# Spreading a value projection over the attention heads that use it, with shorter softmax and norm arithmetic around it

## The chip, the cores and the metric

The kernel runs on one core of one Trainium2 chip. The metric is the device time of one execution in microseconds (us). A core has a matrix engine (TensorE, PE in the profile, with its weight loads as PEld), a vector engine (VectorE, DVE), a scalar engine for table functions (ScalarE, ACT), a general engine (GpSimd, POOL) and a queue that issues the DMA transfers (SyncE, SP). TensorE writes its sums into PSUM, which has 8 banks; VectorE and ScalarE read them from there. Each engine runs its own list of instructions in a fixed order and waits where an instruction's inputs or its output buffer are not ready.

## The reference, cut to what matters

The program is two transformer blocks of the first kind, then one of a second kind, for 512 tokens of width 1024 in float32. The change is in the attention of the second kind, and in one helper that the very first mixer uses too. From the second kind:

```python
xn = rmsnorm_2(h, norm1_w[l])
proj = xn @ w_in[l]
qd, kd, vd, qc, kc, vc, gd, gc = jnp.split(proj, IN_SPLITS, axis=-1)
# differential attention: 8 heads, two maps each, one value of width 128 per head
def probs(qq, kk):
    s = jnp.einsum('bqhd,bkhd->bhqk', qq, kk).astype(f32) * scale + bias
    return jax.nn.softmax(jnp.where(allowed, s, -jnp.inf), axis=-1)
a = probs(qblk[..., 0, :], k1) - lam * probs(qblk[..., 1, :], k2)
o = a @ v                                   # per head
o = rmsnorm_2(o, subln_w) * (1.0 - lam_init) # norm over the head's 128 values
# chunk attention: 8 heads of width 64, each chunk sees itself and the 8 before it
p = jax.nn.softmax(s, axis=-1)
```

Then both outputs are gated, projected and added to the residual, and a retrieval stage (`peer`) follows.

## The kernel before

Every projection is done in float32 by splitting both operands into a high and a low part: a unit of weights (128 x 1024) is loaded by SP (line 236), cast on ScalarE (line 248), its remainder taken on VectorE (line 249), and three TensorE matmuls make each product. The units lie in memory in the order in which the program uses them (`_weight_units`), so a change of order in the program comes with one there. Two helpers use them:

- `ws` (lines 324 to 334) computes one transposed 128 x 512 tile, 24 matmuls of 512 columns into one PSUM bank (lines 320 to 322). In the second mixer the bank is one of the two called `mm`, in turn. Queries and keys are made so.
- `xs` (lines 336 to 353) computes 256 columns for all 512 tokens: two units, 96 matmuls of 256 columns (lines 350 to 352), into two banks at once, both of which are open until the last matmul. `xs_to` (line 355) then copies them out with four ScalarE instructions (line 359), scaled by the row norm `rcol`. Values are made so.

PSUM holds two banks each of `mm`, `pz`, `pa` and `ps`. Attention uses `pz` for the logits (line 975), `ps` for transposes and `pa` for a head's output.

`mixer_2` (line 909) first makes all 1024 columns of the differential values with `xs_to(v, 1024)` (line 951), on `pa` and `pz` in turn. Then a list of generators runs in `pipeline` (line 192): at most `DW` = 3 at a time, a new one at every third step (`DG` = 3). The list follows `ORDER`: eight `diff_head`, one `chunk_values` (two steps of `xs_to` on the `pz` banks for the 512 chunk values), four `chunk_pair`. A `diff_head` makes its query and key (`qk`, line 955) in its first step. In each of four more it makes the logits of 128 queries (line 976), adds the bias and takes the row maximum in one VectorE instruction (line 985), negates the maximum (line 988), takes the exponential with its row sum on ScalarE (line 990), a reciprocal (line 991), combines the two maps (lines 1033 and 1034), and, one step late, transposes the result (line 999), copies it (line 1000) and multiplies it by the values (line 1007). `head_norm` (line 693) closes the head: squares on ScalarE (line 700), `rsqrt` (line 361: 12 small VectorE instructions, a bit pattern as first guess and three Newton steps), scaling (line 707), transposes (line 450). It is used by the four heads of the first mixer (`mixer_ab`) as well.

The order on each engine is not written out: a scheduler places ready instructions, and the program's order decides between them. ScalarE's function tables are loaded by an instruction that the toolchain puts where it is needed; the program names a table set once, in `setup` (line 438), ahead of `mixer_ab`.

Of the kernel before, what the change touches and what calls it, by code (L numbers as in the profile page):

```python
# [35 lines left out]
DW, DG, AG = 3, 3, 5  # L36
MR, KEEP = 2, 20
QB, QK, BB, EB = 2, 2, 4, 7
ORDER = 'ddddddddvcccc'
WIDE = ['mm', 'mm', 'pz', 'pz', 'pa', 'pa']  # L40
G_MIX0, G_FFN0, G_PLE0, G_MIX1, G_FFN1, G_PLE1, G_N1, G_N2 = range(8)

# [31 lines left out]
def _weight_units(i):  # L74
    us = []
    ab = i['ab_w_in'][0]
    fq = _interleave(_ws_units(ab[:, 2048:2560]), _ws_units(ab[:, 1536:2048]),
                     _ws_units(ab[:, 0:512]), _ws_units(ab[:, 512:1024]))
    gs = _xs_units(ab[:, 3072:3584], 256)
    us += gs[:2] + fq[:4] + gs[2:]  # L80
    us += _xs_units(ab[:, 1024:1536], 256)
    us += _xs_units(ab[:, 2560:3072], 256)
    us += fq[4:]
    us += _ws_units(i['ab_w_out'][0])

    def ffn(l):
        r = []
        for a, b in PIECES:
            r.extend(_interleave(_ws_units(i['ffn_up'][l], range(a, b)),
                                 _ws_units(i['ffn_up'][l], range(NF + a, NF + b))))  # L90
            r.extend(_ws_units(i['ffn_down'][l], None, a, b))
        return r

    def ple(l):
        pr = _pack(_ws_units(i['ple_proj'][l]), 4)
        ga = _ws_units(i['ple_gate'][l])
        return [pr[0]] + ga[:4] + [pr[1]] + ga[4:]

    us += ffn(0) + ple(0)
    cw = i['c_w_in'][0]  # L100
    us += _xs_units(cw[:, 1280:1536], 256)
    k_cols = cw[:, 1024:1280]
    q_idx = np.concatenate([np.arange(64) + 64 * (8 * P + 4 * a + g)
                            for P in range(2) for g in range(4) for a in range(2)])
    kt = _ws_units(k_cols)
    qt = _ws_units(cw[:, q_idx])
    us += [kt[0], kt[1]] + qt
    us += _ws_units(i['c_w_out'][0][q_idx, :])
    us += ffn(1) + ple(1)
    w2 = i['w_in_2'][0]  # L110
    us += _xs_units(w2[:, 2048:3072], 256)
    diff = _interleave(_ws_units(w2[:, 0:1024]), _ws_units(w2[:, 1024:2048]))
    values = _xs_units(w2[:, 4096:4608], 256)
    chunk = _interleave(_ws_units(w2[:, 3072:3584]), _ws_units(w2[:, 3584:4096]))
    for kind in ORDER:
        part, n = {'d': (diff, 2), 'v': (values, len(values)), 'c': (chunk, 2)}[kind]
        us += part[:n]
        del part[:n]
    gd = _ws_units(w2[:, 4608:5632])
    gc = _ws_units(w2[:, 5632:6656])  # L120
    bd = _ws_units(i['w_branch_diff_2'][0])
    bc = _ws_units(i['w_branch_chunk_2'][0])
    for m in range(8):
        us += [gd[m], gc[m], bd[m], bc[m]]
    us += _ws_units(i['w_out_2'][0])
    us += _ws_units(i['peer_wq_2'][0])
    return us
# [132 lines left out]
class Kernel:  # L260
# [100 lines left out]
    def rsqrt(self, src, n, scale):  # L361

        nc = self.nc
        new = lambda name, dtype=F32: self.sm.tile([128, 8], dtype, name=name)[:, :n]
        ms, iy = new("rq_m"), new("rq_i", I32)
        nc.vector.tensor_scalar(ms, src, scale, EPS, op0=ALU.mult, op1=ALU.add)
        nc.vector.tensor_scalar(iy, ms.bitcast(I32), 1, None, op0=ALU.logical_shift_right)
        nc.vector.tensor_scalar(iy, iy, -1, 0x5F3759DF, op0=ALU.mult, op1=ALU.add)
        y = iy.bitcast(F32)
        for r in range(3):  # L370
            t, yn = new("rq_t"), new("rq_y")
            nc.vector.tensor_mul(t, y, y)
            nc.vector.scalar_tensor_tensor(t, t, -0.5, ms, op0=ALU.mult, op1=ALU.mult)
            nc.vector.scalar_tensor_tensor(yn, t, 1.5, y, op0=ALU.add, op1=ALU.mult)
            y = yn
        return y


    def norm_k(self, k, g, first=False, to=None):
# [313 lines left out]
    def head_norm(self, tmp, po, gain, y, scale=None):  # L693

        nc = self.nc
        o = tmp.tile([128, T], F32, name="fp")
        ss = tmp.tile([128, 4], F32, name="hn_s")
        for tb in range(4):
            s = slice(tb * 128, tb * 128 + 128)
            nc.scalar.activation(o[:, s], po[:, s], AF.Square, accum_out=ss[:, tb:tb + 1],  # L700
                                 scale=1.0 if scale is None else scale[:, tb:tb + 1])
        r = self.rsqrt(ss, 4, 1.0 / 128)
        if scale is not None:
            nc.vector.tensor_mul(r, r, scale)
        for tb in range(4):
            s = slice(tb * 128, tb * 128 + 128)
            nc.vector.scalar_tensor_tensor(o[:, s], po[:, s], r[:, tb:tb + 1], gain[:, tb, :],
                                           op0=ALU.mult, op1=ALU.mult)
        self.transpose4(o, self.yh[:, y], self.yl[:, y])
# [199 lines left out]
    def mixer_2(self):  # L909
# [3 lines left out]
        with ExitStack() as outer:  # L913
# [3 lines left out]
            with ExitStack() as st:  # L917
# [30 lines left out]
                v = self.const([128, 4, 1024], "h")  # L948
                v2 = one.tile([128, 4, 512], F32, name="v2")
                self.norm_end()  # L950
                self.xs_to(v, 1024)

                kz = self.zeros(one, QB)

# [22 lines left out]
                        pl.append(ps)  # L977
                    return pl

                def probs(pl, tb, bias, r):  # L980

                    n = 128 * (tb + 1)
                    e = tmp.tile([128, T], F32, name="e", bufs=EB)
                    mx = tmp.tile([128, 1], F32, name="mx", bufs=8)
                    nc.vector.tensor_tensor_reduce(out=e[:, :n], in0=pl[:, :n], in1=bias[:, T - n:], scale=1.0,
                                                   scalar=-3.0e38, op0=ALU.add, op1=ALU.max, accum_out=mx)
                    ng = tmp.tile([128, 1], F32, name="ng", bufs=8)
                    nc.vector.tensor_scalar(ng, mx, -1.0, None, op0=ALU.mult)
                    z = tmp.tile([128, 1], F32, name="z", bufs=10)
                    nc.scalar.activation(e[:, :n], e[:, :n], AF.Exp, bias=ng, accum_out=z)  # L990
                    nc.vector.reciprocal(r, z)
                    return e[:, :n], z

                def turned(e, tb):
                    n = 128 * (tb + 1)
# [23 lines left out]
                def diff_head(h):  # L1019
                    q, k = qk()  # L1020
                    bias = tmp.tile([128, T], F32, name="bias", bufs=BB)
                    nc.vector.tensor_scalar(bias, nd, 2.0 ** -(h + 1), None, op0=ALU.mult)
                    yield
                    po = self.pa.tile([128, T], F32, name="pa")
                    last = None

                    r4 = tmp.tile([128, 4], F32, name="r4", bufs=3)
                    for tb in range(4):
                        r2 = tmp.tile([128, 1], F32, name="r", bufs=8)
                        pl = logits(q, k, tb)  # L1030
                        e1, z1 = probs(pl[0], tb, bias, r4[:, tb:tb + 1])
                        e2, _ = probs(pl[1], tb, bias, r2)
                        nc.vector.scalar_tensor_tensor(r2, r2, nlam, z1, op0=ALU.mult, op1=ALU.mult)
                        nc.vector.scalar_tensor_tensor(e1, e2, r2, e1, op0=ALU.mult, op1=ALU.add)
                        if last is not None:
                            values(po, *last, slice(h * 128, h * 128 + 128))
                        last = (e1, tb)
                        yield
                    values(po, *last, slice(h * 128, h * 128 + 128))
                    self.head_norm(tmp, po, sb4, h, r4)  # L1040

                def chunk_values():
                    for c in range(0, 512, 256):
                        self.xs_to(v2[:, :, c:c + 256], 256, "pz")
                        yield

                def chunk_pair(hp):
                    q, k = qk()
                    biases = []
                    for a in range(2):  # L1050
                        bias = tmp.tile([128, T], F32, name="bias", bufs=BB)
                        nc.sync.dma_start(bias, self.i['chb'][2 * hp + a])
                        biases.append(bias)
                    yield
                    po = self.pa.tile([128, T], F32, name="pa")
                    last = None
                    for tb in range(4):
                        pl = logits(q, k, tb)
                        es = []
                        for a in range(2):  # L1060
                            r = tmp.tile([128, 1], F32, name="r", bufs=8)
                            e, _ = probs(pl[a], tb, biases[a], r)
                            nc.vector.tensor_scalar(e, e, r, None, op0=ALU.mult)
                            es.append(e)
                        if last is not None:
                            values2(po, *last, hp * 128)
                        last = (es, tb)
# [1 line left out]
                    values2(po, *last, hp * 128)  # L1069
                    self.split(y2h[:, hp], y2l[:, hp], po)  # L1070

                parts = {'d': map(diff_head, range(8)), 'v': iter([chunk_values()]), 'c': map(chunk_pair, range(4))}
                pipeline([next(parts[kind]) for kind in ORDER], DW, DG)
                self.h = self.const([128, KD, T], "h")
                for a in range(KD):
                    nc.sync.dma_start(self.h[:, a, :], hd[a])
# [380 lines left out]
```

## Time and profile before

| what | us |
|---|---|
| median of 3 runs (3294.6 to 3304.15) | 3296.83 |
| the profiled execution, its own time | 3298.76 |
| its span in the trace | 3296.7 |
| TensorE busy in it | 3172.2 (96%) |
| VectorE busy | 2333.6 (71%) |
| ScalarE busy | 1457.9 (44%) |

The mean granted TensorE clock of the execution is 0.988 of full speed. The second mixer's attention lies between about 1440 and 1790 us. A busy share of TensorE is a modelled one: a matmul that waits in the pipeline counts as busy, so the number of matmuls in a stretch says more than the share.

### The profile page before, as it was taken

How to read it: one execution, taken by the hardware profiler on the slowest of the kernel's cores; microseconds unless marked ns; L12 is line 12 of the kernel's file. 1: busy time of each engine (PE TensorE's matmuls, PEld its weight loads, DVE VectorE, ACT ScalarE, POOL GpSimd, SP SyncE). 2: the span in 40 equal slices, each digit the busy share in tenths (PEclk: the TensorE clock that was granted, in tenths of full speed). 3: DMA queues.
4: the chain of work that ended last, by engine and by line, in shares of the span. 5: the costliest groups of instructions: out<-in, count | busy, mean ns of one | idle time of the engine just before them, and what ended most of it. 6: DMA issues, size and time to landing. Idle time of an engine off the chain costs nothing.

```text
span 3296.7 us, 44324 instructions
## 1 busy us (share of the span) xinstructions
PE 3172.2 (96%) x16121; PEld 2663.3 (81%) x16121; DVE 2333.6 (71%) x4667; ACT 1457.9 (44%) x2606; POOL 642.0 (19%) x640
## 2 busy tenths in 40 slices
PE   8998999999999999999799999999999999889998
PEld 7876877878778778798587888999999898667786
DVE  7687746566666466667855457999999788788654
ACT  5565323333444233345655233366767433233333
POOL 4234100022230000220000020021245444333000
PEclk9999999999999999999899999999999999999999
DMA  3211222223112222232131333567799999999762
GB/s 117 71 52 59 91 95 90 96 90 115 39 40 90 96 87 98 91 118 77 42 100 60 97 103 104 165 235 273 258 330 340 371 336 333 344 350 358 255 200 83
DMA packets 202762, 523.48 MB, mean 159 GB/s; under 512 B 17968, under 2 KB 91312, under 8 KB 201008
## 3 DMA queue, kind: packets, MB, share of 16 engines
q1 hardware_dynamic: 165680, 386.42, 34.8%
q0 software_dynamic: 36864, 134.23, 11.2%
q8 instruction: 127, 2.08, 0.3%
q14 instruction: 91, 0.75, 0.1%
HBM read 474.71 MB, written 45.88 MB: 158 GB/s over the span
## 4 chain that ended last, share of the span: by engine, by line
PE 85%; DVE 9%; DMA 2%; ACT 2%; issue 2%; POOL 0%; SPq 0%; DVEq 0%; ACTq 0%; POOLq 0%
PE mm L322 11%; PE mm L320 11%; PE mm L321 11%; PE pz L1363 5%; PE pa L1363 5%; PE ps L1363 5%; PE pz L322 4%; PE pz L320 4%; PE pz L321 4%; PE pa L322 4%; PE pa L320 4%; PE pa L321 4%; DVE wlo L249 2%; PE ps L1293 1%; DMA u<-in_pu,e 1%
## 5 line engine op out<-in xcount | busy, mean ns | idle before, releaser
L248 ACT CAST whi<-wr 128x1024 fp32r<-128x1024 f32 (+2 forms) x435 | 448.9, 1034 | 812.5 <-PE mm L321 338.9
L249 DVE TENSOR_TENSOR wlo<-wr,whi 128x1024 fp32r<-128x1024 f32 (+2 forms) x435 | 554.4, 1276 | 174.8 <-ACT whi L248 172.0
L322 PE MATMUL mm<-yh,wlo 128*128 128x384 f32 (+1 forms) x1260 | 450.0, 358 | 11.9 <-DVE wlo L249 11.4
L320 PE MATMUL mm<-yh,whi 128*128 128x384 f32 (+1 forms) x1260 | 449.2, 357 | 6.8 <-ACT whi L248 3.5
L321 PE MATMUL mm<-yl,whi 128*128 128x384 f32 (+1 forms) x1260 | 447.3, 355 | 0.0
L322 PEld LDWEIGHTS mm<-yh,wlo 128*128 128x128 f32 x1260 | 238.3, 189 | 33.9 <-DVE wlo L249 18.1
L320 PE MATMUL mm<-xh,whi 128*128 128x512 f32 x652 | 260.1, 401 | 4.7 <-DVE q L958 3.4
L321 PE MATMUL mm<-xl,whi 128*128 128x512 f32 x652 | 260.8, 400 | 0.0
L322 PE MATMUL mm<-xh,wlo 128*128 128x512 f32 x652 | 260.2, 400 | 0.0
L320 PEld LDWEIGHTS mm<-yh,whi 128*128 128x128 f32 x1260 | 238.1, 189 | 25.8 <-ACT whi L248 5.9
L321 PEld LDWEIGHTS mm<-yl,whi 128*128 128x128 f32 x1260 | 238.3, 189 | 15.5 <-DVE yl L287 0.4
L1147 POOL DMA_INDIRECT u<-in_pv,e x128 | 176.0, 1375 | 239.7 <-DVE hacc L1154 131.2
L1147 POOL DMA_INDIRECT u<-in_pu,e x128 | 166.8, 1303 | 209.7 <-DVE hid L1151 119.4
L286 ACT CAST ah<-a 128x384 fp32r<-128x384 f32 x128 | 65.5, 513 | 229.4 <-PE ps L1363 136.4
L1154 DVE SCALAR_TENSOR_TENSOR hacc<-u,hid,hacc 128x1024 f32<-128x1024 f32 x128 | 163.7, 1279 | 0.6
L1151 DVE CUSTOM_DVE_ANT_0 u<-u,xt 128x1024 f32<-128x1024 f32 x128 | 155.0, 1222 | 10.0 <-DMA u<-in_pu,e 10.0
L320 PEld LDWEIGHTS mm<-xh,whi 128*128 128x128 f32 x652 | 122.5, 189 | 36.6 <-DVE q L958 3.6
L322 PEld LDWEIGHTS mm<-xh,wlo 128*128 128x128 f32 x652 | 123.0, 189 | 30.4 <-issue 1.6
L321 PEld LDWEIGHTS mm<-xl,whi 128*128 128x128 f32 x652 | 123.0, 189 | 28.8 <-issue 1.0
L287 DVE TENSOR_TENSOR al<-a,ah 128x384 fp32r<-128x384 f32 x128 | 71.0, 556 | 103.3 <-ACT ah L286 94.9
L742 POOL MEMSET un<- 128x2 f32 x88 | 8.6, 99 | 663.2 <-DVE cv L748 605.2
L1289 DVE TENSOR_SCALAR o<-io,tr 128x128 f32<-128x128 f32 x384 | 109.3, 358 | 0.1
(495 smaller groups left out, 7646.6 us busy)
## 6 DMA issues: line engine op xcount, KB each, us to landing
wr<-in_wall SPq DMA_DIRECT2D x256, 512.0 KB, 3.3
wr<-in_ut SPq DMA_DIRECT2D x116, 512.0 KB, 5.2
xh<-in_pv SPq DMA_DIRECT2D x72, 512.0 KB, 5.7
wr<-in_pv SPq DMA_DIRECT2D x56, 512.0 KB, 5.5
G<-Gd SPq DMA_DIRECT2D x32, 768.0 KB, 8.4
Hd<-hg SPq DMA_DIRECT2D x84, 192.0 KB, 3.4
hg<-Hd SPq DMA_DIRECT2D x84, 192.0 KB, 6.0
wr<-in_wall SPq DMA_DIRECT2D x32, 448.0 KB, 3.3
```

The source lines that it names most:

```text
L248: k.nc.scalar.copy(hi[:, :ln], r)
L249: k.nc.vector.tensor_tensor(lo[:, :ln], r, hi[:, :ln].bitcast(F32), op=ALU.subtract)
L286: self.nc.scalar.copy(hi, src)
L287: self.nc.vector.tensor_sub(lo, src, hi.bitcast(F32))
L320: mm(ps, w[0], x[0], start=first, stop=False)
L321: mm(ps, w[0], x[1], start=False, stop=False)
L322: mm(ps, w[1], x[0], start=False, stop=last)
L1147: tc.keep_in_program_order(nc.gpsimd.indirect_dma_start(out=u, out_offset=None, in_=self.i[table], in_offset=bass.IndirectOffsetOnAxis(ap= ...
L1151: nc.vector.tensor_tensor_reduce(out=u, in0=u, in1=xt, scale=1.0, scalar=0.0, op0=ALU.mult, op1=ALU.add, accum_out=hid[:, j:j + 1])
L1154: nc.vector.scalar_tensor_tensor(hacc[:, 0], u, hid[:, j:j + 1], hacc[:, 0], op0=ALU.mult, op1=ALU.add)
L1289: nc.vector.tensor_scalar(o2[:, j], io, tr[:, 1, t + j:t + j + 1], tr[:, 2, t + j:t + j + 1], op0=ALU.is_equal, op1=ALU.mult)
L1363: mm(accs[b][c], w[:, ts], r[:, c * 512:c * 512 + 512], start=n == 0 and r is hi and w is ah, stop=n == 127 and w is al)
```

## The change

The differential values are no longer made ahead: every second `diff_head` makes 256 columns, those of itself and the next head, right after its query and key, on the two `mm` banks. Every second `chunk_pair` does the same for the chunk values, and the generator `chunk_values` goes. The units lie in the new order. The line at 985 now yields the negated logits and the negated maximum (scale -1, minimum), so line 988 goes and the exponential takes scale -1. Reciprocals are taken once for four row sums (`r4`) or for two (chunk pairs). `head_norm` uses a new `rsqrt_ln`, with logarithm and exponential on ScalarE for the first guess and one Newton step.

```diff
+    for part, vals, n in ((diff, dv, 8), (chunk, values, 4)):
+        for h in range(n):
+            us += part[2 * h:2 * h + 2]
+            if h % 2 == 0:
+                us += vals[h:h + 2]
...
+    def rsqrt_ln(self, src, n, scale):
+        nc = self.nc
+        new = lambda name: self.sm.tile([128, 8], F32, name=name)[:, :n]
+        ms, y, t, r = new("rq_m"), new("rl_y"), new("rq_t"), new("rq_y")
+        nc.vector.tensor_scalar(ms, src, scale, EPS, op0=ALU.mult, op1=ALU.add)
+        nc.scalar.activation(y, ms, AF.Ln)
+        nc.scalar.activation(y, y, AF.Exp, scale=-0.5)
+        nc.vector.tensor_mul(t, y, y)
+        nc.vector.scalar_tensor_tensor(t, t, -0.5, ms, op0=ALU.mult, op1=ALU.mult)
+        nc.vector.scalar_tensor_tensor(r, t, 1.5, y, op0=ALU.add, op1=ALU.mult)
+        return r
...
-        r = self.rsqrt(ss, 4, 1.0 / 128)
+        r = self.rsqrt_ln(ss, 4, 1.0 / 128)
...
-                self.xs_to(v, 1024)
...
-                def probs(pl, tb, bias, r):
+                def probs(pl, tb, bias, z):
...
-                    mx = tmp.tile([128, 1], F32, name="mx", bufs=8)
-                    nc.vector.tensor_tensor_reduce(out=e[:, :n], in0=pl[:, :n], in1=bias[:, T - n:], scale=1.0,
-                                                   scalar=-3.0e38, op0=ALU.add, op1=ALU.max, accum_out=mx)
                     ng = tmp.tile([128, 1], F32, name="ng", bufs=8)
-                    nc.vector.tensor_scalar(ng, mx, -1.0, None, op0=ALU.mult)
-                    z = tmp.tile([128, 1], F32, name="z", bufs=10)
-                    nc.scalar.activation(e[:, :n], e[:, :n], AF.Exp, bias=ng, accum_out=z)
-                    nc.vector.reciprocal(r, z)
-                    return e[:, :n], z
+                    nc.vector.tensor_tensor_reduce(out=e[:, :n], in0=pl[:, :n], in1=bias[:, T - n:], scale=-1.0,
+                                                   scalar=3.0e38, op0=ALU.add, op1=ALU.min, accum_out=ng)
+                    nc.scalar.activation(e[:, :n], e[:, :n], AF.Exp, scale=-1.0, bias=ng, accum_out=z)
+                    return e[:, :n]
...
+                    if h % 2 == 0:
+                        self.xs_to(v[:, :, h * 128:h * 128 + 256], 256, "mm")
                     yield
...
-                        e1, z1 = probs(pl[0], tb, bias, r4[:, tb:tb + 1])
-                        e2, _ = probs(pl[1], tb, bias, r2)
+                        e1 = probs(pl[0], tb, bias, z1)
+                        e2 = probs(pl[1], tb, bias, z2)
+                        nc.vector.reciprocal(r2, z2)
...
                     values(po, *last, slice(h * 128, h * 128 + 128))
+                    nc.vector.reciprocal(r4, z4)
                     self.head_norm(tmp, po, sb4, h, r4)
...
+                    if hp % 2 == 0:
+                        self.xs_to(v2[:, :, hp * 128:hp * 128 + 256], 256, "mm")
...
+                        es = [probs(pl[a], tb, biases[a], z[:, a:a + 1]) for a in range(2)]
+                        nc.vector.reciprocal(z, z)
...
-                pipeline([next(parts[kind]) for kind in ORDER], DW, DG)
+                pipeline([diff_head(h) for h in range(8)] + [chunk_pair(hp) for hp in range(4)], DW, DG)
```

## Rows read from the trace of the kernel before

**Rows 1.** Second mixer's windows: length, busy (instructions) PE, PEld, DVE, ACT, POOL, clock, DMA.
```profile
1440.00:1484.00 44.00, 44.00 (x371) 43.59 (x371) 14.41 (x36) 16.40 (x27) 0.00 (x0) 1.00 0.28 94
1484.00:1540.00 56.00, 56.00 (x268) 46.33 (x267) 39.82 (x111) 31.26 (x68) 0.00 (x0) 1.00 0.26 85
1540.00:1610.00 70.00, 62.41 (x312) 51.00 (x310) 55.99 (x200) 43.80 (x106) 0.00 (x0) 0.95 0.19 61
1610.00:1650.00 40.00, 25.47 (x130) 19.87 (x131) 35.61 (x171) 27.09 (x90) 0.00 (x0) 0.79 0.06 20
...
1700.00:1790.00 90.00, 90.00 (x530) 69.02 (x530) 55.50 (x191) 53.04 (x128) 0.00 (x0) 1.00 0.19 59
```

**Rows 2.** Windows of tile mm's instructions alone: the same columns without POOL.
```profile
1610.00:1650.00 40.00, 0.00 (x0) 0.00 (x0) 1.36 (x2) 0.00 (x0) 0.79 0.06 20
```

**Rows 3.** Groups by form on PE, 1540 to 1700: count, busy, mean, idle before.
```profile
L320 PE MATMUL mm<-xh,whi 128*128 128x512 f32 x80 | 33.2, 415 | 3.5 <-DVE q L958 3.4
...
L1007 PE MATMUL pa<-h,eT 128*128 128x128 f32 x140 | 21.5, 286 | 1.7 <-ACT eT L1000 1.4
L350 PE MATMUL pz<-whi,xh 128*128 128x256 f32 x64 | 19.6, 307 | 2.1 <-DVE mx L985 2.0
...
L999 PE MATMUL ps<-ident,e 128*128 128x128 f32 x70 | 13.3, 293 | 0.0
L306 PE MATMUL pz<-kt,qh 128*128 128x256 f32 x24 | 8.0, 342 | 6.6 <-DVE mx L985 6.6
L306 PE MATMUL pz<-kt,qh 128*128 128x512 f32 x13 | 6.9, 530 | 4.5 <-DVE mx L985 3.5 <-ACT v L359 1.0
...
L450 PE MATMUL ps<-ident,fp 128*128 128x128 f32 x28 | 6.5, 325 | 0.0
...
L306 PE MATMUL pz<-kt,qh 128*128 128x384 f32 x12 | 5.0, 418 | 4.8 <-DVE mx L985 4.8
```

**Rows 4.** Chain that ended last, in time: start, us of the chain, work.
```profile
1486.19 0.23 PE mm L320
...
1535.11 0.89 PE pa L1007 x8
```

**Rows 5.** Groups on DVE and ACT, 1440 to 1790.
```profile
L991 DVE RECIPROCAL r<-z 128x1 f32<-128x1 f32 x96 | 14.9, 159 | 12.2 <-ACT e L990 11.4
L988 DVE TENSOR_SCALAR ng<-mx 128x1 f32<-128x1 f32 x96 | 13.3, 147 | 0.5
...
L963 DVE TENSOR_TENSOR q<-mm,rbc 128x512 f32<-128x512 f32 x12 | 8.2, 687 | 5.2 <-PE mm L322 5.1
...
L373 DVE SCALAR_TENSOR_TENSOR rq_t<-rq_t,rq_m 128x4 f32<-128x4 f32 x27 | 4.3, 161 | 0.5
...
L932 ACT ACTIVATE l<-l 128x2 f32<-128x2 f32 x1 | 0.2, 204 | 0.0
```

**Rows 6.** Timeline on ACT: the copy of rbc, a copy-out of values.
```profile
1451.80 0.59 ACT L420 COPY rbc<-ps 128x512 f32<-128x512 f32 x1 [1.09 <-PE ps L417]
...
1680.75 1.57 ACT L359 ACTIVATE v<-pz,rcol 128x256 f32<-128x256 f32 x4
```

**Rows 7.** Waits, 1440 to 1790: us in total, times, longest.
```profile
PE mm L320 <- DVE q L958: 3.4, 1, 3.4
...
DVE rq_m L366 <- ACT fp L700: 4.6, 5, 2.6
```

**Rows 8.** Waits of SP's own queue, same columns.
```profile
SPq L1052 <- DVE r L1033: 15.7, 1, 15.7
```

**Rows 9.** Groups of table loads on ACT, whole span.
```profile
L438 ACT ACT_TABLE_LOAD x1 | 1.3, 1283 | 0.8 <-PEq L1447 0.8
...
L932 ACT ACT_TABLE_LOAD x1 | 1.3, 1283 | 3.8 <-DVE rq_m L366 3.8
```

**Rows 10.** Timeline of a table load on ACT and the instruction behind it.
```profile
2064.43 1.28 ACT L1137 ACT_TABLE_LOAD   x1
2065.73 0.49 ACT L1137 ACTIVATE hg<-mm 128x384 f32<-128x384 f32 x1
```

More of the change, by code (lines that the diff above doesn't have):

```diff
@@ L38 @@
 QB, QK, BB, EB = 2, 2, 4, 7
-ORDER = 'ddddddddvcccc'
 WIDE = ['mm', 'mm', 'pz', 'pz', 'pa', 'pa']
@@ L110, in _weight_units @@
     w2 = i['w_in_2'][0]
-    us += _xs_units(w2[:, 2048:3072], 256)
     diff = _interleave(_ws_units(w2[:, 0:1024]), _ws_units(w2[:, 1024:2048]))
+    dv = _xs_units(w2[:, 2048:3072], 256)
     values = _xs_units(w2[:, 4096:4608], 256)
     chunk = _interleave(_ws_units(w2[:, 3072:3584]), _ws_units(w2[:, 3584:4096]))
[L115 to L118, printed above, removed]
+    for part, vals, n in ((diff, dv, 8), (chunk, values, 4)):
[3 more added lines that the diff above has]
+                us += vals[h:h + 2]
     gd = _ws_units(w2[:, 4608:5632])
@@ L1025, in diff_head @@
                     last = None
-                    r4 = tmp.tile([128, 4], F32, name="r4", bufs=3)
+                    z4 = tmp.tile([128, 4], F32, name="z4", bufs=3)
                     for tb in range(4):
+                        z1, z2 = z4[:, tb:tb + 1], tmp.tile([128, 1], F32, name="z", bufs=8)
+                        pl = logits(q, k, tb)
+                        e1 = probs(pl[0], tb, bias, z1)
+                        e2 = probs(pl[1], tb, bias, z2)
                         r2 = tmp.tile([128, 1], F32, name="r", bufs=8)
-                        pl = logits(q, k, tb)
-                        e1, z1 = probs(pl[0], tb, bias, r4[:, tb:tb + 1])
-                        e2, _ = probs(pl[1], tb, bias, r2)
+                        nc.vector.reciprocal(r2, z2)
                         nc.vector.scalar_tensor_tensor(r2, r2, nlam, z1, op0=ALU.mult, op1=ALU.mult)
@@ L1039, in diff_head @@
                     values(po, *last, slice(h * 128, h * 128 + 128))
+                    r4 = tmp.tile([128, 4], F32, name="r4", bufs=3)
+                    nc.vector.reciprocal(r4, z4)
                     self.head_norm(tmp, po, sb4, h, r4)
[L1042 to L1045, printed above, removed]
                 def chunk_pair(hp):
@@ L1058, in chunk_pair @@
                         pl = logits(q, k, tb)
-                        es = []
+                        z = tmp.tile([128, 2], F32, name="z2", bufs=8)
+                        es = [probs(pl[a], tb, biases[a], z[:, a:a + 1]) for a in range(2)]
+                        nc.vector.reciprocal(z, z)
                         for a in range(2):
[L1061 to L1064, printed above, removed]
+                            nc.vector.tensor_scalar(es[a], es[a], z[:, a:a + 1], None, op0=ALU.mult)
                         if last is not None:
@@ L1070, in chunk_pair @@
                     self.split(y2h[:, hp], y2l[:, hp], po)
-                parts = {'d': map(diff_head, range(8)), 'v': iter([chunk_values()]), 'c': map(chunk_pair, range(4))}
-                pipeline([next(parts[kind]) for kind in ORDER], DW, DG)
+                pipeline([diff_head(h) for h in range(8)] + [chunk_pair(hp) for hp in range(4)], DW, DG)
                 self.h = self.const([128, KD, T], "h")
```

## The prediction

> **What bounds the kernel now.** I read the page first: TensorE is busy 96% of the span, so nearly everywhere only what leaves TensorE without work can be won. Then I cut the second mixer into windows [rows 1]. The reader is to look at the number of matmuls in each, not at the busy share. From 1440 to 1484, where the values are made, and from 1484 to 1540 TensorE is full at full clock. From 1610 to 1650 it issues 130 matmuls in 40 us, while VectorE is busy 35.6 us, and the granted clock is 0.79, that is partly the lower level of 1.2 GHz. The windows of the `mm` banks alone [rows 2] say why: there is not one query or key projection in that stretch. `chunk_values` stands in the list between the last head and the first chunk pair, writes to the `pz` banks that the logits hold, and the three places of the pipeline are taken; what is left for TensorE are logits, transposes and value products, each of which waits for VectorE or ScalarE.
>
> How much is lost follows from the groups by form of 1540 to 1700 [rows 3] and the spacing of matmuls where nothing waits. A 512-column one takes 0.233 us, eight of 128 columns 0.89 us, so 0.111 each [rows 4]; one of 256 columns takes 44/371 = 0.119 us [rows 1]. Three lines of 80 projections make 240 x 0.233 = 55.9 us, three lines of 64 value matmuls 192 x 0.119 = 22.8, the 140 + 70 + 28 products and transposes 238 x 0.111 = 26.4, the logits (two lines of each form) 48 x 0.119 + 26 x 0.233 + 24 x 0.176 = 16.0; 0.176 is the middle of the two spacings. Together 121.1 us of work in 160 us: **38.9 us are lost**. The last two sums are 336 matmuls at 0.126 us; the 130 of 1610 to 1650 are then 16.4 us of work, and 23.6 us of the loss lie there, 15.3 elsewhere in the 160 us. This is the pool from which the change can draw; the waits in it stand in the idle columns of [rows 3], for `pz` banks held by VectorE's line 985 above all.
>
> **The change part by part.** *The move of the values.* 12 units of value matmuls, 8 from the front and 4 from the `pz` stretch, become six blocks of 96 x 0.119 = 11.4 us behind the projections of heads 0, 2, 4, 6 and chunk pairs 0 and 2. Their matmuls, casts, remainders and four copies per block are the same as before; only their place is new. The front loses 44 us, and the heads gain TensorE work that waits for no softmax. The loss of 1610 to 1650 (23.6 us) is the size of a chunk pair's projections (48 x 0.233 = 11.2) and one block (11.4) together, which now can stand there: I count it as gone. Of the other 15.3 us I count half as gone, as the waits for VectorE there stay but shrink: -38.9 + 7.7.
>
> *The price of the `mm` banks.* A block opens both `mm` banks at once. Its first matmuls must wait until the key has been taken out of its bank by line 963, 0.69 us [rows 5], and the next head's query waits for two of the block's four copies, 1.57/2 = 0.8 us [rows 6]. Behind the waiting matmul in TensorE's queue stand the logits and transposes of the other heads; behind the copies in ScalarE's queue stand exponentials and the copies of transposes. Bare, that is 1.5 us a block. Where VectorE or ScalarE has other work first, it is more: one wait of a query for its `mm` bank took 3.4 us before [rows 7], and with all four copies that makes 5.0. Bounds for six blocks: 0 (other heads' matmuls placed in the gap) to 30. I take 1.2 a block, near the bare price less some cover: +7.
>
> *The start.* Head 0's query now needs `rbc` before its bank comes free; `rbc` is copied at 1451.8 to 1452.4 [rows 6], and the two projections of 11.2 us that begin about 1440 end at 1451. Bounds 0 to 3, taken +1.5.
>
> *Queues.* SP issues as many transfers as before. Chunk pair 0's two bias loads now stand ahead of the weight loads that follow its values; such a load can hold the queue long, 15.7 us once [rows 8], but the block's two units are asked for three units ahead, by the key's. Cost 0 while that lead holds; without it a block waits for its load.
>
> *Smaller arithmetic.* On VectorE 96 negations of 0.147 us go [rows 5], 13.3 us; of 96 reciprocals 56 are left, 40 x 0.159 = 6.4 us; a norm has 4 instructions in place of 12, 8 x 0.161 = 1.3 us, for 8 heads 10.3 us. Together 30 us, of some 200 that VectorE is busy in the windows of [rows 1]. VectorE is not the bound of a mixer in which TensorE is fed, so this counts for nothing of its own: it is part of why half of the 15.3 us go. If TensorE's cover fails, as from 1610 to 1650 before, it is worth up to 30 us. In the first mixer four norms shorten; I take -1, between 0 and -5.2 (4 x 1.3).
>
> *Tables.* The new norm asks ScalarE for a logarithm and an exponential, about 0.2 us each by the nearest row, an exponential of 128 x 2 [rows 5]. The program names a set of tables only at line 438. That one load serves the whole first mixer, where logarithm and exponential alternate; in the second mixer a load was placed at line 932 for an exponential alone [rows 9]. No row shows whether that set holds the logarithm. If not, each norm of the second mixer loads twice: 16 x 1.283 = 20.5 us of ScalarE. The load takes 1.28 us and the next instruction starts 0.02 us after it [rows 10]. In the dense window from 1610 to 1650 ScalarE was busy 27.1 of 40 us [rows 1], so most of a load falls into free time. Bounds: 0 to 45 (the rival below); I hold the loads for likelier than not, as nothing asks for the joint set there, and take +5.
>
> The Trainium skill, page ScalarE: Activation LUTs, section Table sets: the hidden batching unit, counts one load for a logarithm followed by an exponential, from a set that has both; with that at line 932 the loads would be none, and the sum 5 us lower. Section What ACT_TABLE_LOAD costs of the same page gives 2.66 us a switch, a drain of 1.38 us with it; 16 of these would be 42.6 us of ScalarE. The row just named does not show the drain.
>
> **The sum.** -38.9 + 7.7 + 7 + 1.5 + 5 - 1 = -18.7 us. From the profiled execution's 3298.8 that is 3280.1; the median of the runs is 1.9 us lower, so 3278.
>
> **The rivals.** *A, the forecast*, chance 0.45: 3278, its own range 3266 to 3287.
>
> *B, more of the pool*, 0.20: line 932's set has both functions, the gaps of the `mm` banks are filled by other heads, and a quarter of the 15.3 us stays. -38.9 + 3.8 + 1.5 - 1 = -34.6: 3262. For it: where projections were at hand, 1484 to 1540, TensorE lost nothing [rows 1]. Against it: six places where both banks change hands. The table rule of the Trainium skill named above would help it; no row here decides on that.
>
> *C, the banks take what the stretch gives*, 0.20: each block pays the 5.0 us of the queued case. -38.9 + 7.7 + 30 + 1.5 + 5 - 1 = +4.3: 3301, no change. For it: the 3.4 us wait [rows 7] came with one bank at stake, here it is two. Against it: it came once in twelve heads and pairs.
>
> *D, slower: the norm halts ScalarE*, 0.15: the order of instructions is fixed, so ScalarE stands at the logarithm until VectorE has the mean, which itself waits for the squares, up to 2.6 us [rows 7], and with two loads and two small functions (2.57 + 0.4) up to 5.6 us a norm, with the exponentials of the other heads behind it and VectorE's Newton step waiting. 8 x 5.6 = 45: -38.9 + 7.7 + 7 + 1.5 + 45 - 1 = +21.3: 3318. It decides from 4.2 us a norm on TensorE's path, where the sum passes +9.9. For it: ScalarE's waits for VectorE are the long ones here. Against it: a block or a pair of projections (11 us) outlasts it, if placed there.
>
> **Range and chances.** 0.3% of 3296.8 is 9.9 us, about what a measurement of this kernel can tell from no change. A and B lie below 3287: faster 0.65. C lies between 3287 and 3307: same 0.20. D: slower 0.15. The range for 8 in 10 reaches from 3256, just under B, to 3304, over C; it leaves out most of D and a case in which the whole pool is won.
>
> **What would show it.** The 44 us of value matmuls at the front are gone and their lines write to `mm`; no window of 40 us in the attention is without `mm` matmuls; waits of line 306 for line 985 shrink from 6.6 + 3.5 + 4.8 = 14.9 us [rows 3] to a few; the clock stays near 1.00. New waits: line 350 for line 963, line 320 for line 359, about 1 us each. Table loads at the new norm's lines: 16 or none. The prediction is wrong if TensorE stands still behind the copies or the norm for more than 5 us a time, or if the stretch without projections only moves to another place, such as the end of the chunk pairs.

## The result and the profile after

The kernel after takes 3273.34 us (median of 6 runs, 3265.62 to 3285.24) against 3299.86 for the kernel before in the same session (6 runs, 3294.6 to 3304.15). The ratio is 0.9923, 95% interval 0.9908 to 0.9938: faster by about 25 us. The forecast was 3278, with a range from 3256 to 3304 and a chance of 0.65 for faster. The profiled execution took 3274.98 us, its span is 3273.2.

The first part of the page after, busy time of each engine, its share and its instructions:

```profile
PE 3165.9 (97%) x16121; PEld 2660.5 (81%) x16121; DVE 2309.6 (71%) x4435; ACT 1482.8 (45%) x2646; POOL 640.9 (20%) x640
```

TensorE's busy time hardly changed (3172.2 before); the span around it shrank. Where it shrank is shown by the second mixer's windows of the kernel after, which answer to [rows 1] (length, busy and instructions of PE, PEld, DVE, ACT, POOL, granted clock, DMA share, GB/s):

```profile
1440.00:1484.00 44.00, 39.44 (x225) 34.85 (x224) 25.35 (x66) 18.20 (x35) 0.00 (x0) 0.92 0.26 83
1484.00:1540.00 56.00, 55.76 (x332) 48.89 (x331) 39.55 (x108) 41.72 (x94) 0.00 (x0) 1.00 0.21 66
1540.00:1610.00 70.00, 68.75 (x458) 61.95 (x457) 50.70 (x148) 56.15 (x134) 0.00 (x0) 1.00 0.22 72
1610.00:1650.00 40.00, 40.00 (x248) 35.63 (x247) 29.80 (x85) 29.79 (x73) 0.00 (x0) 1.00 0.23 79
...
1700.00:1790.00 90.00, 86.06 (x479) 63.83 (x478) 39.23 (x97) 42.92 (x93) 0.24 (x1) 0.98 0.19 59
```

The stretch from 1610 to 1650 has gone from 130 matmuls at clock 0.79 to 248 at 1.00, and 1540 to 1610 from 312 to 458. In exchange the first window lost what it had: 39.44 of 44 us busy, clock 0.92. (The stage ends earlier, so the last line reaches beyond the attention.) From the last residual add before the mixer to the first copy of a gate, in the timeline of VectorE, the stage took 354.1 us before (1437.4 to 1791.5) and 328.6 after (1441.4 to 1770.0): all of the 25 us are there.

The windows of the `mm` banks alone in the kernel after answer to [rows 2] (no POOL column):

```profile
1540.00:1580.00 40.00, 30.11 (x166) 24.17 (x165) 2.73 (x4) 1.55 (x4) 1.00 0.21 68
...
1610.00:1650.00 40.00, 31.84 (x156) 24.62 (x155) 2.74 (x4) 0.00 (x0) 1.00 0.23 79
...
1690.00:1730.00 40.00, 24.74 (x127) 19.60 (x126) 1.38 (x2) 1.57 (x4) 1.00 0.21 67
1730.00:1770.00 40.00, 8.20 (x34) 5.87 (x32) 0.00 (x1) 0.00 (x0) 1.00 0.11 34
```

Projections and values now run in every stretch, least in the last 40 us. PE's groups by form from 1540 to 1700 in the kernel after, to be read against [rows 3]:

```profile
L321 PE MATMUL mm<-xh,whi 128*128 128x512 f32 x100 | 39.8, 398 | 0.0
...
L351 PE MATMUL mm<-whi,xh 128*128 128x256 f32 x122 | 33.6, 281 | 0.0
...
L1017 PE MATMUL pa<-h,eT 128*128 128x128 f32 x120 | 17.2, 275 | 0.0
L1009 PE MATMUL ps<-ident,e 128*128 128x128 f32 x76 | 13.6, 276 | 0.0
L307 PE MATMUL pz<-kt,qh 128*128 128x256 f32 x27 | 8.3, 308 | 0.0
...
L464 PE MATMUL ps<-ident,fp 128*128 128x128 f32 x28 | 6.1, 281 | 1.9 <-DVE fp L721 1.9
L307 PE MATMUL pz<-kt,qh 128*128 128x384 f32 x14 | 5.4, 384 | 0.0
...
L307 PE MATMUL pz<-kt,qh 128*128 128x512 f32 x12 | 4.7, 391 | 0.0
L1025 PE MATMUL pa<-eT,v 128*64 128x128 f32 x14 | 2.4, 294 | 0.0
```

The logits' idle columns, 14.9 us before, are 0.0. An estimate by the prediction's own spacings: 300 projections, 366 value matmuls, 238 products and transposes and two lines of each form of logits make 156.8 us of work in these 160 us, so 3.2 are lost where 38.9 were before. What TensorE still waits for, from 1440 to 1800 (us in total, times, longest), answers to the first line of [rows 7]:

```profile
PE ps L431 <- DVE rcol L423: 3.2, 1, 3.2
PE ps L464 <- DVE fp L721: 2.1, 4, 0.6
PE pa L321 <- DVE sg L1101: 2.0, 1, 2.0
PE mm L351 <- DVE q L971: 1.4, 1, 1.4
```

The first and the last of these are the start; the third belongs to the stage behind. The timeline of that moment in the kernel after (start, us, engine and line, what it waited for), to be read against the first of [rows 6]:

```profile
1454.60 1.13 PE L431 MATMUL ps<-ident,rcol 128*128 128x128 f32 x8 [3.16 <-DVE rcol L423]
1455.77 0.59 ACT L434 COPY rbc<-ps 128x512 f32<-128x512 f32 x1 [3.48 <-PE ps L431]
1456.38 0.69 DVE L971 SCALAR_TENSOR_TENSOR q<-mm,rbc 128x512 f32<-128x512 f32 x1 [1.93 <-ACT rbc L434]
...
1457.13 0.58 PE L351 MATMUL mm<-whi,xh 128*128 128x256 f32 x1 [1.40 <-DVE q L971]
```

Both `mm` banks hold head 0's query and key, which cannot leave without `rbc`, so the first block waits for both. Before, value matmuls on `pa` and `pz` filled that time.

ScalarE's groups of table loads in the kernel after answer to [rows 9]:

```profile
L385 ACT ACT_TABLE_LOAD x8 | 10.3, 1283 | 0.1
L386 ACT ACT_TABLE_LOAD x8 | 10.3, 1283 | 0.1
...
L946 ACT ACT_TABLE_LOAD x1 | 1.3, 1283 | 4.7 <-DVE l L945 4.7
```

The new norm loads twice in each of the second mixer's eight norms and never in the first mixer. One norm on ScalarE's timeline:

```profile
1505.60 1.28 ACT L385 ACT_TABLE_LOAD   x1
1506.89 0.20 ACT L385 ACTIVATE rl_y<-rq_m 128x4 f32<-128x4 f32 x1
1507.12 1.28 ACT L386 ACT_TABLE_LOAD   x1
1508.41 0.20 ACT L386 ACTIVATE rl_y<-rl_y 128x4 f32<-128x4 f32 x1
```

The logarithm starts when the load has ended, 0.01 us later, as in [rows 10]. VectorE meanwhile stands at the Newton step. Its wait in the kernel after, 1440 to 1800:

```profile
DVE rq_t L387 <- ACT rl_y L386: 20.7, 8, 2.9
```

### The profile page after: what moved, and what is told of

Its sections match the earlier page's. It is cut to its first block, busy times and chain, and to the rows that moved or that the text cites. A ratio compares the mean times of both kernels' runs of the same rounds, so it can differ in the third digit from the quotient of the medians.

```text
span 3273.2 us, 44121 instructions
## 1 busy us (share of the span) xinstructions
PE 3165.9 (97%) x16121; PEld 2660.5 (81%) x16121; DVE 2309.6 (71%) x4435; ACT 1482.8 (45%) x2646; POOL 640.9 (20%) x640
## 3 DMA queue, kind: packets, MB, share of 16 engines
q0 software_dynamic: 36864, 134.23, 11.2%
## 4 chain that ended last, share of the span: by engine, by line
PE 85%; DVE 9%; DMA 2%; ACT 2%; issue 2%; POOL 0%; SPq 0%; DVEq 0%; ACTq 0%; POOLq 0%
PE mm L323 11%; PE mm L321 11%; PE mm L322 11%; PE pz L1374 5%; PE ps L1374 5%; PE pa L1374 5%; PE pz L323 4%; PE pz L321 4%; PE pz L322 4%; PE pa L323 4%; PE pa L321 4%; PE pa L322 4%; DVE wlo L250 2%; PE ps L1304 1%; PE mm L351 1%
## 5 line engine op out<-in xcount | busy, mean ns | idle before, releaser
L323 PEld LDWEIGHTS mm<-xh,wlo 128*128 128x128 f32 x652 | 122.6, 188 | 29.7 <-issue 1.6
```

The source lines that it names most:

```text
L323: mm(ps, w[1], x[0], start=False, stop=last)
```

## The experiments

Eleven kernels, each timed beside the kernel before on the same chip; differences are (ratio - 1) x 3300 us. The ratio is not the quotient of the two medians; the two differ by up to 0.001, some 3 us. An interval of 0.0014 to either side is some 4.6 us, so differences of less than about 6 between two kernels are not separated by the times alone. The last column is the length of the stage, taken as above, in the one profiled execution of each kernel; it leaves out what the rest of the program adds to the time, but a single execution has no interval.

| kernel | median us (runs) | ratio [95%] | us | stage us |
|---|---|---|---|---|
| before | 3299.86 (6) | 1 | 0 | 354.1 |
| after | 3273.34 (6) | 0.9923 [0.9908, 0.9938] | -25.4 | 328.6 |
| e2 move only | 3271.25 (6) | 0.9919 [0.9904, 0.9933] | -26.7 | 328.2 |
| e4 chunk values only | 3283.76 (8) | 0.9959 [0.9946, 0.9972] | -13.5 | 347.8 |
| e8 differential values only | 3283.77 (6) | 0.9948 [0.9935, 0.9962] | -17.2 | 336.4 |
| e3 arithmetic only | 3302.2 (12) | 1.001 [0.9999, 1.0021] | +3.3 | 358.8 |
| e3b the same, joint tables | 3288.72 (10) | 0.9969 [0.996, 0.9979] | -10.2 | 347.4 |
| e1 after, joint tables | 3267.88 (5) | 0.99 [0.9885, 0.9914] | -33.0 | 324.8 |
| e5 after, old norm | 3268.2 (5) | 0.991 [0.9897, 0.9923] | -29.7 | 327.5 |
| e7 after, loads doubled | 3294.0 (12) | 0.9983 [0.9973, 0.9993] | -5.6 | 354.3 |
| e6 after, blocks on pz | 3286.07 (6) | 0.9965 [0.9953, 0.9977] | -11.6 | 343.8 |
| e9 e1, first block ahead | 3260.38 (4) | 0.9878 [0.9864, 0.9893] | -40.3 | 317.7 |
| e10 e9, old norm | 3263.1 (5) | 0.9898 [0.9884, 0.9912] | -33.7 | 323.9 |

### The move and the arithmetic apart

**Move only.** The kernel before with both values moved, all arithmetic as it was.

```diff
...
-                self.xs_to(v, 1024)
...
+                    if h % 2 == 0:
+                        self.xs_to(v[:, :, h * 128:h * 128 + 256], 256, "mm")
                     yield
...
+                    if hp % 2 == 0:
+                        self.xs_to(v2[:, :, hp * 128:hp * 128 + 256], 256, "mm")
...
```

> The kernel before with the values moved to the heads and chunk pairs, on the mm banks, and nothing else: old maximum, old reciprocals, old norm. If the gain comes from projections that fill the stretch without them, this alone gains 15 to 24 us on the kernel before. If the gain comes from VectorE's shorter arithmetic, it gains under 8 us, or loses by the banks.

It gave -26.7 us, as much as the whole change and somewhat more than the 15 to 24 expected. The arithmetic, table loads included, adds nothing visible to the kernel after.

**Arithmetic only.** The kernel after with the move taken back: values at the front, `chunk_values` on `pz`.

```diff
+                self.xs_to(v, 1024)
...
-                    if h % 2 == 0:
-                        self.xs_to(v[:, :, h * 128:h * 128 + 256], 256, "mm")
                     yield
...
-                pipeline([diff_head(h) for h in range(8)] + [chunk_pair(hp) for hp in range(4)], DW, DG)
+                pipeline([diff_head(h) for h in range(8)] + [chunk_values()] + [chunk_pair(hp) for hp in range(4)], DW, DG)
```

> The kernel before with the new arithmetic only (negated maximum, merged reciprocals, norm by logarithm and exponential) and the values where they were. If the projections' place makes the gain, this gains 3 to 12 us, as VectorE has 30 us less and the stretch of 40 us without projections stays. If VectorE is what bounds that stretch and its work is the cause, it gains 18 us or more. If the table loads cost their time where nothing covers them, it gains nothing.

It gave +3.3 us with an interval that reaches to no change. Its window of the starved stretch:

```profile
1610.00:1650.00 40.00, 25.11 (x127) 19.61 (x126) 30.36 (x103) 34.02 (x89) 0.00 (x0) 0.79 0.09 31
```

Against [rows 1] VectorE has 5.25 us less to do there and ScalarE 6.93 more, and TensorE gets no more matmuls (127 for 130) and no better clock. Among TensorE's waits of this kernel, 1435 to 1800, is one that the kernel before does not have, at the transposes behind the norm:

```profile
PE ps L458 <- DVE fp L715: 6.8, 3, 3.9
```

To see whether the table loads ate the gain, the same kernel with one set for both functions:

```diff
+                self.tc.keep_in_program_order(nc.scalar.preload_act_table_set("natural_log_exp_and_others"))
                 nc.scalar.activation(l2, l2, AF.Exp)
```

> The new arithmetic with the values where they were, and the joint table set asked for before the second mixer's first exponential, so no loads at the norms. With the loads this was level with the kernel before. If the loads ate the gain of the shorter VectorE work in the stretch where TensorE has no projections, this gains 8 us or more on the kernel before. If VectorE's work does not set that stretch, it stays within 4 us of it.

The 16 loads are gone and the time is 13.5 us below that of e3; the intervals do not touch. The wait behind the norm falls from 6.8 to 1.2 us. Smaller arithmetic is worth 10.2 us in the kernel whose stretch is still starved, and the loads took all of it.

### The two halves of the move

Only the chunk values moved, then only the differential ones; the rest as before.

```diff
...
+    us += dv
...
+        if h % 2 == 0:
+            us += values[h:h + 2]
...
+                    if hp % 2 == 0:
+                        self.xs_to(v2[:, :, hp * 128:hp * 128 + 256], 256, "mm")
...
```

> The kernel before with the chunk values alone moved into chunk pairs 0 and 2, on the mm banks; the differential values stay at the front, the arithmetic stays. If the loss lies in the stretch that the generator of the chunk values makes (23.6 us), this gains 12 to 24 us on the kernel before. If the differential values at the front are what is missing behind the heads, it gains under 8 us.

```diff
...
+        if h % 2 == 0:
+            us += dv[h:h + 2]
+    us += values
...
-                self.xs_to(v, 1024)
...
+                    if h % 2 == 0:
+                        self.xs_to(v[:, :, h * 128:h * 128 + 256], 256, "mm")
...
```

> The kernel before with the differential values alone moved to the heads, on the mm banks; the generator of the chunk values on the pz banks and the old arithmetic stay. The chunk values alone gained 13 us, both together 27. If the two moves add up, this gains 8 to 18 us. If the stretch made by the generator must go first, it gains under 5 us; if the differential values alone fill the gaps behind the heads, 20 us or more.

-13.5 and -17.2, together -30.7; both moved at once give -26.7. So the halves nearly add, and neither contains the other. How the gain divides between them is less sure: their medians are equal, and the profiled stages are 6.3 and 17.7 us shorter than before. Windows of the kernel with the chunk values moved:

```profile
1540.00:1610.00 70.00, 61.89 (x306) 50.56 (x305) 55.64 (x197) 43.72 (x109) 0.00 (x0) 0.94 0.19 64
1610.00:1650.00 40.00, 37.93 (x234) 34.23 (x233) 31.78 (x129) 24.16 (x70) 0.00 (x0) 0.93 0.14 47
...
1720.00:1760.00 40.00, 38.05 (x236) 26.14 (x235) 28.07 (x123) 27.53 (x81) 0.00 (x0) 0.91 0.15 47
```

The starved stretch filled (234 matmuls), but the tail, full before at clock 1.00 [rows 1], now has 38.05 of 40 us at 0.91 from 1720 to 1760: part of the gain is given back there. Windows of the kernel with the differential values moved:

```profile
1540.00:1610.00 70.00, 70.00 (x460) 63.43 (x459) 56.28 (x197) 45.12 (x115) 0.00 (x0) 1.00 0.26 83
1610.00:1650.00 40.00, 33.77 (x203) 29.94 (x202) 26.53 (x114) 22.10 (x64) 0.00 (x0) 0.87 0.10 34
```

Here `chunk_values` is still on `pz`, yet the window before the stretch is full and the stretch has 203 matmuls. That count mixes two things, as this kernel's stage begins 5.6 us later than before and its heads are spread otherwise. The stretch without `mm` matmuls is still there, but shorter. The windows of the `mm` banks alone, first in the kernel before and then in this one:

```profile
1610.00:1680.00 70.00, 0.00 (x0) 0.00 (x0) 1.36 (x2) 0.00 (x0) 0.85 0.12 38
1620.00:1660.00 40.00, 0.00 (x0) 0.00 (x0) 0.50 (x1) 0.00 (x0) 0.87 0.13 42
```

Within it TensorE starves for 20 us, at 0.79 as before, until the generator's value matmuls come:

```profile
1620.00:1640.00 20.00, 13.77 (x70) 11.41 (x69) 16.14 (x73) 12.08 (x36) 0.00 (x0) 0.79 0.12 41
```

Moving the chunk values does two things at once: it changes their bank, and it frees the place that their generator took among the three of the pipeline. No run takes these apart.

### The table loads

**Joint tables.** The line added in e3b, in the kernel after.

> The changed kernel with one more instruction: the second mixer asks for the table set with both logarithm and exponential before its first exponential. The 16 table loads at the new norm go. If the loads fall into time in which TensorE has projections to work on (the forecast's term of 5 us), the kernel ends 0 to 7 us before the changed one, some 3267 to 3273. If each norm halts ScalarE on TensorE's path (rival D), at least the 20.5 us of the loads come back, 3253 or less.

-33.0, 7.6 us below the kernel after; the two intervals overlap by a hair (0.9908 to 0.9914). VectorE's wait for the norm there, 1440 to 1800:

```profile
DVE rq_t L387 <- ACT rl_y L386: 1.5, 3, 0.5
```

20.7 us have become 1.5.

**The old norm.** The kernel after with its first guess and Newton steps on VectorE again.

```diff
-        r = self.rsqrt_ln(ss, 4, 1.0 / 128)
+        r = self.rsqrt(ss, 4, 1.0 / 128)
```

> The changed kernel with the old norm (bit pattern and three Newton steps on VectorE) in both mixers; values, maximum and reciprocals as changed. It has no table loads for norms. If the 16 loads are what the changed kernel still pays (the kernel with the joint table set gained some 5 us on it), this gains as much, 3265 to 3270. If the new norm's shorter VectorE work is worth something by itself, this stays at the changed kernel's 3273 or above.

-29.7, between the kernel after and e1; its interval overlaps both. By the ratios the new norm costs 4.3 us as it stands and saves 3.3 with joint tables; these pairs do not prove either.

**Loads doubled.** A rival had the norm's loads halt the kernel. To see how far that is off, each norm alternates twice, which gives 32 loads in place of 16 and 16 more small functions of 0.2 us. Of the 32, 28 stand at the norm and 4 at the exponential of a softmax (line 1004) that the scheduler placed inside a norm's chain.

```diff
-        nc.scalar.activation(y, ms, AF.Ln)
-        nc.scalar.activation(y, y, AF.Exp, scale=-0.5)
+        y0 = new("rl_0")
+        nc.scalar.activation(y0, ms, AF.Ln)
+        nc.scalar.activation(y0, y0, AF.Exp, scale=-1.0)
+        nc.scalar.activation(y, y0, AF.Ln)
+        nc.scalar.activation(y, y, AF.Exp, scale=0.5)
```

> The changed kernel with the norm's first guess made by two logarithms and two exponentials in a chain, so 32 table loads in the second mixer in place of 16, and four small ScalarE functions a norm in place of two. The joint table set, which takes the 16 loads away, gained some 7 us. If a load costs about the same wherever TensorE is fed, the second 16 cost 5 to 10 us. If ScalarE has now no free time left, the cost nears the bare 20.5 us of the loads or more.

-5.6: the second 16 loads cost 19.8 us (0.9923 to 0.9983), almost all of their own length, 20.5 us. Waits of this kernel, 1440 to 1800:

```profile
PE ps L467 <- DVE fp L724: 11.1, 5, 4.1
PE mm L321 <- ACT v L360: 4.2, 1, 4.2
...
DVE rq_t L390 <- ACT rl_y L389: 30.7, 6, 6.6
```

TensorE now stands at the transposes behind the norm (11.1 us, 2.1 in the kernel after), and once a query waits 4.2 us for a block's copies. This profile is that of a run of 3284.22 us, the shortest of the twelve, but what made it short lies outside the stage: the stage itself took 354.3 us, 25.7 more than in the kernel after.

### The banks and the start

**Blocks on pz.** The kernel after with the six blocks on the logits' banks, in place of the projections'.

```diff
-                        self.xs_to(v[:, :, h * 128:h * 128 + 256], 256, "mm")
+                        self.xs_to(v[:, :, h * 128:h * 128 + 256], 256, "pz")
```

> The changed kernel with the six blocks of values on the pz banks of the logits in place of the projections' mm banks. Blocks on pz keep the logits of all heads from their banks for 11 us each. If the projections' banks matter for the gain, this loses 10 us or more on the changed kernel. If only the place in the order matters, it stays within 5 us.

-11.6: 13.9 us worse than on `mm`. Its windows:

```profile
1440.00:1484.00 44.00, 43.25 (x253) 37.67 (x252) 29.99 (x73) 22.75 (x43) 0.08 (x1) 1.00 0.30 95
1540.00:1610.00 70.00, 65.22 (x410) 57.61 (x410) 45.93 (x139) 51.17 (x125) 0.00 (x0) 0.95 0.17 57
1610.00:1680.00 70.00, 66.10 (x383) 57.97 (x382) 43.60 (x115) 45.87 (x107) 0.00 (x0) 0.93 0.24 78
```

TensorE has gaps and the clock falls in the heads, where the kernel after has 68.75 of 70 us at 1.00. While a block is open, no head can write logits. TensorE's longest wait in total is then 4.3 us for the copies of transposes (line 1010), which it does not wait for in the kernel after; that late logits cause it is argued from the order of the program. At the start the bank helps: head 0's block is at the same place as in the kernel after, but need not wait for the query's bank, and the first window is nearly full at 1.00. So the loss in the heads is larger than 13.9 us, by what the start gives (next run).

**First block ahead.** e1, with head 0's block made before its query and key, on `pz`, which nothing else holds yet.

```diff
...
+                    if h == 0:
+                        self.xs_to(v[:, :, 0:256], 256, "pz")
...
-                    if h % 2 == 0:
+                    if h % 2 == 0 and h:
                         self.xs_to(v[:, :, h * 128:h * 128 + 256], 256, "mm")
```

> The changed kernel with the joint table set, and with head 0's block of values ahead of its query and key, on the pz banks, as it needs no row norm until it is copied out. The changed kernel's trace shows TensorE waiting 3.2 + 1.4 us at the start for the norm and then for the query's bank, at a granted clock of 0.89. If that wait is on the path, this gains 4 to 7 us on the kernel with the joint set alone. If the wait only moves (the first logits come 11 us later), it gains nothing.

-40.3, 7.3 us below e1 with intervals that overlap at their edge. Its first window, to be read against the kernel after's:

```profile
1440.00:1484.00 44.00, 44.00 (x250) 38.15 (x250) 29.98 (x70) 21.59 (x38) 0.00 (x0) 1.00 0.29 95
```

TensorE is full from the start at clock 1.00: the 4.56 us of idle time and the lower clock are gone. By the median it is the fastest kernel of the study.

**The same with the old norm** and no named set of tables (in e9, `rsqrt` for `rsqrt_ln`).

> Head 0's block of values ahead of its query and key, as in the kernel that did so with the joint table set, but with the old norm in both mixers. If the new norm with the joint set is worth nothing where TensorE is fed, this is level with that kernel, 3257 to 3264; if it is, this is 3 us or more slower.

-33.7, 4.0 below e5, which has the same norm and the old start, and 6.6 above e9, which has the same start. The start is therefore put at 4 to 7.3 us from two pairs, neither of which is beyond its intervals alone; the profiled stages differ by 3.6 and 7.1 us. Against e9 the new norm with joint tables saves 6.6 us, beside the 3.3 from e5 and e1; this too stays within the intervals, and the two expectations of this run are not told apart.

## Why the prediction held, step by step

The ratios of e2, e1 and after lead from one term to the next: the move -26.7, arithmetic without loads -6.3, loads +7.6, together -25.4. The prediction had -22.7 for the move's four terms, nothing for the arithmetic of the second mixer, +5 for the tables and -1 for the first mixer. That its sum of -18.7 came so near is in part luck: the banks were put 7 us too dear and the start 2.5 to 5.8 too cheap, and the arithmetic gave 6.3 us more and the tables took 2.6 more than forecast, so the errors partly cancel.

- **The fill** (-38.9 + 7.7 = -31.2) held in size. The move alone gave -26.7; less the 4 to 7.3 us that the start costs, and with hardly a wait for banks, it is -31 to -34 as a remainder; the count of work in the rows from 1540 to 1700 above gives 35.7 of the 38.9 us, as an estimate. So half of the 15.3 us was a cautious share. Its place was only half right. The prediction put 23.6 us into 1610 to 1650 and took the missing projections there as the cause, with the other 15.3 as waits that shrink. e8 leaves `chunk_values` where it was, and the stretch without projections still shrinks from 70 us and more to some 40; e4 fills it and wins 13.5, with a loss at the tail in return. In these runs the pool belongs to the whole stage, and either half of the move took some of it.
- **The `mm` banks** (+7) were mis-sized: no wait for a block's copies stands among TensorE's in the kernel after, and the only one behind a query is the 1.4 us at the start. The predicted waits of 1 us a block did not appear, as in the lower bound, where other heads' matmuls fill the gap. The bank does cost nearly what rival C priced (5.0 us) when the copy is late: 4.2 us, once, in e7.
- **The start** (+1.5, bounds 0 to 3) was mis-sized the other way, and its bound too low: 4 to 7.3. The prediction let head 0's projections begin "about 1440", an edge of a window and no start of anything. TensorE's timeline of the kernel before has the stage's first matmul at 1434.33:

```profile
1434.33 0.40 PE L350 MATMUL pa<-whi,xh 128*128 128x256 f32 x2
```

and that of the kernel after the first of head 0's query at 1438.29:

```profile
1438.29 0.40 PE L321 MATMUL mm<-xh,whi 128*128 128x512 f32 x1
```

The copy of `rbc` starts 17.5 us behind it in both (1451.80 - 1434.33, 1455.77 - 1438.29). From there the prediction's own working gives 17.5 + 0.6 - 11.2 = 6.9 us without a free bank. e9 and e6 show that this one block is the cause: with it on `pz`, ahead of the query (e9) or behind the key as before (e6), the first window has no wait for `rcol` or for the query's bank.
- **Queues** (0) held. SP's own queue waits at the bias loads in the kernel after as it did in [rows 8]:

```profile
SPq L1063 <- DVE ng L999: 25.1, 5, 10.4
```

but no wait of TensorE in the attention is for a late unit by more than the 1.1 us of one remainder (line 250).
- **Smaller arithmetic** (nothing of its own, up to 30 if the cover fails): measured -6.3 under the move (not separated by its intervals) and -10.2 without it. That it is worth little while TensorE is fed is right in kind; zero may have been too low. VectorE's busy time fell by 24.0 us in the whole kernel, less than the 30 that the prediction counted for the second mixer alone.
- **The first mixer** (-1): no difference was found between the traces up to there, nor was it run by itself. In the profiled executions the six kernels with the old norm end the block ahead of the second mixer at 1435.1 to 1443.0 us, the six with the new one at 1441.3 to 1447.9 (e7, with four small functions, at 1435.6): no gain is to be seen there. Left open.
- **Tables** (+5): the loads came, 16 of 1.283 us, as held likelier, and cost 7.6 us under the move (after and e1, whose intervals just overlap) and 13.5 without it (e3 and e3b).

Of the rivals, B needed the joint set: with it the kernel is at -33.0, close to B's -34.6, but by other terms: B had nothing for the arithmetic, and its start was too cheap. Its gaps at the banks did not show as waits, as it had them. C did not occur. D saw the right mechanism, VectorE waiting for the loads, and it does stand there 2.6 us a norm, but the wait hardly passes on to TensorE (2.1 us in all); twice the loads bring it to TensorE. ScalarE itself did not stand at the logarithm, as D had it: it waited for the mean (line 384) once, 0.2 us.

The Trainium skill, page ScalarE: Activation LUTs, section Table sets: the hidden batching unit, counts a logarithm followed by an exponential as one load. The trace disagrees for this kernel as it is built: two loads a norm, because nothing asks for the set that holds both; with that set named (e1) there are none at the norm.

## What to carry to other kernels

A stretch in which TensorE waits on softmax was filled here with matmuls that depend on no softmax and use banks that the softmax doesn't hold; the same blocks on the logits' banks gave back 14 of 25 us. When work is moved off the front of a stage, look at what it covered there: the chain of the row norm became visible, and one block put where its bank was free was worth 4 to 7 us. When a function is moved to ScalarE, count table loads in the trace and name a set that holds all functions of the stage.

## What was not expected of the hardware

- Loads do not cost in proportion. 16 loads cost 7.6 us in the kernel after, the next 16 cost 19.8, with each load at 1283 ns in both. The profiled stages say the same: 3.8 and 25.7 us.
- Loads on ScalarE stopped VectorE for 20.7 us, while TensorE waited 2.1 us behind the norm: the cost stood first at the engine whose next instruction needed the result, and reached TensorE (11.1 us) with twice the loads.
- The granted clock was lower in windows with gaps, but not in all of them: 0.92 in the first window of the kernel after, with 4.56 us idle in 44, and 0.95 and 0.93 with blocks on `pz`, with 4.8 and 3.9 us idle in 70. With the loads doubled a window of 5.4 us idle kept 1.00:

```profile
1540.00:1610.00 70.00, 64.61 (x419) 57.15 (x418) 49.30 (x142) 55.15 (x126) 0.00 (x0) 1.00 0.21 72
```

- The second mixer begins between 1435.1 and 1447.9 us, in kernels that differ ahead of it by no more than the norm's arithmetic; with the old norm alone it is 1435.1 to 1443.0. One profile of each does not say why. Windows at the same time in two kernels can be off by that much, so lengths of the stage are to be trusted more.
